# LayerNorm on channels: two transposes of the token's numbers in place of four transposes back

## The chip, the cores and the metric

The kernel runs on one core of one Trainium2 chip. A core has a matrix engine (TensorE, PE), three engines for elementwise work (VectorE or DVE, ScalarE or ACT, GpSimd or POOL) and SyncE (SP), which here issues all DMAs. PE writes to PSUM, eight banks of 128 partitions by 512 fp32 words; the others work mainly in SBUF. The metric is the device time of one execution in microseconds (us).

## What is computed

One layer of an encoder. 16 meta tokens stand ahead of the tokens; a prompt of 256 tokens and a sample of 2048 are handled as 18 blocks of 128. One projection makes the parts q, k, v, an attention gate, and for the convolution a value, a gate and an output gate, 512 channels each. The part that the change touches is this:

```
def layernorm(x, w, b):
    mu = jnp.mean(xf, axis=-1, keepdims=True)
    var = jnp.mean(jnp.square(xf - mu), axis=-1, keepdims=True)
    y = (xf - mu) * lax.rsqrt(var + LN_EPS)
    return y * w + b
def conformer_conv(c_val, c_glu, conv_w, conv_b, ln_w, ln_b):
    u = c_val * jax.nn.sigmoid(c_glu)
    y = lax.conv_general_dilated(u, conv_w, ...) + conv_b     # 31 taps, each channel by itself
    return jax.nn.silu(layernorm(y, ln_w, ln_b))              # over the 512 channels of a token
def hybrid_layer(z, ...):
    q, k, v, g_att, c_val, c_glu, g_conv = jnp.split(rmsnorm(z) @ w_in, ...)
    att = windowed_gqa(rmsnorm(q), rmsnorm(k), v, sink) * jax.nn.silu(g_att)
    cnv = conformer_conv(c_val, c_glu, ...) * jax.nn.silu(g_conv)
    return z + jnp.concatenate([att, cnv], axis=-1) @ w_out
```

## The kernel before

**Projection.** The columns of the input projection are cut into units of 256 (weights `ws`), the tokens into groups of 384 (group 0 has 400), and the groups into two chunks of three. Every product is made of three fp32r passes over high and low halves (`xh`, `xl`), so that one unit for one block of 128 tokens is 24 matmuls of 256 columns, `pj73` for instance (L879). Results go through eight PSUM banks under four tags, "a" to "d", with two banks each; a tag's tiles take its two banks in turn, in the order in which the program asks for them.

**Preparing a group of tokens.** The tokens of a group lie transposed in DRAM. Four loads on SP (L743, `xt4_0` to `xt4_3` for group 4) bring 256 channels each. The token's rstd is spread over the partitions by three transposes of a broadcast column (L755, `bc4`, PSUM tag "c"), eight DVE instructions multiply with it (L772, two for each load), ACT casts to `xh` (L791), and DVE and POOL make `xl` (L801). A load into a buffer waits for the `xl` of the group before.

**Convolution and LayerNorm.** DVE adds the 31 taps with the channels on the partitions (L937, L946), into four tiles `y{c}_{j}` of 128 channels each for chunk c. When a chunk is done, `ln_block` handles its blocks: 0 to 7 after chunk 0, 8 to 17 after chunk 1. For a block, step `s1` turns the four pieces of y to tokens on partitions (four transposes, `lnt`, tag "c", L221), DVE makes mean and variance (`bs`, L224; `mv`, L225), and POOL from these rstd and −mean·rstd, columns 1 and 2 of `mv` (L148, L149, L227). `s2` lets DVE write (y · rstd − mean · rstd) from PSUM to `zn` (L234). `s3` turns that back with four transposes (`lnu`, tag "d", or "a" in the attention phase, L240); ACT applies weight, bias and Silu per channel (L243), and SP stores the block to DRAM (`cd`, L246). The last block columns of chunk 0 wait in `ycarry` and are copied ahead of chunk 1's y by ACT.

**What sets the order.** The program goes through the projection's work items; after each, `tick` advances a clock, starts the next LayerNorm block or convolution taps for the time that PE has been given, and runs what `later(k, f)` put off by k ticks. The framework then orders the instructions of each engine itself by a simulated timeline (POOL, and in the attention phase PE, keep the program's order) and puts in the waits that data and buffers need. In a row each engine works strictly in order: an instruction that waits holds all behind it. q leaves PSUM through DVE (`qs`, L1010), and the splits of weights (L839, `wor` L345) run between.

Of the kernel before, what the change touches and what calls it, by code (L numbers as in the profile page):

```python
# [32 lines left out]
NJ = 4  # L33
# [66 lines left out]
def hymba_kernel(  # L100
# [11 lines left out]
    nc = tc.nc  # L112
# [3 lines left out]
    psum = ctx.enter_context(tc.tile_pool(name="psum", bufs=2, space=bass.MemoryType.PSUM))  # L116
# [45 lines left out]
    def later(k, f):  # L162
        due.setdefault(clock[0] + k, []).append(f)
# [45 lines left out]
    phase = [1]  # L209

    def ln_block(c, b, ready):
        if c == 0:
            o = P * b if b < NB_P else 286 + P * (b - NB_P)
        else:
            o = P * (b - 8)
        st = {}

        def s1():
            pt = psum.tile([P, 512], F32, tag="c", name=f"lnt{b}")
            for j in range(NJ):  # L220
                nc.tensor.transpose(pt[:, P * j : P * j + P], yt[c, j][:, o : o + P], ident)  # L221
            bs = yp.tile([P, 6], F32, tag="bs", name=f"bs{b}")
            mv = yp.tile([P, 3], F32, tag="mv", name=f"mv{b}")
            nc.vector.bn_stats(out=bs, in_=pt)  # L224
# [3 lines left out]
            st["pt"], st["mv"] = pt, mv  # L228
            later(1, s2)

        def s2():
            st["zn"] = yp.tile([P, 512], F32, tag="zn", name=f"zn{b}", bufs=3)
            mv = st["mv"]
            nc.vector.tensor_scalar(st["zn"], st["pt"], mv[:, 1:2], mv[:, 2:3], op0=ALU.mult, op1=ALU.add)  # L234
            later(1, s3)

        def s3():
            pt = psum.tile([P, 512], F32, tag="d" if phase[0] == 1 else "a", name=f"lnu{b}")
            for j in range(NJ):
                nc.tensor.transpose(pt[:, P * j : P * j + P], st["zn"][:, P * j : P * j + P], ident)  # L240
            cn = st["zn"].rearrange("p (j n) -> p j n", n=P)
            for j in range(NJ):
                nc.scalar.activation(  # L243
                    cn[:, j, :], pt[:, P * j : P * j + P], AF.Silu, bias=lb[:, j : j + 1], scale=lw[:, j : j + 1]
                )
            later(1, lambda: nc.sync.dma_start(cd[b], st["zn"]))  # L246

        ln_q.append((ready, s1))

# [450 lines left out]

    if True:
        rows0 = {}
        sq0 = yp.tile([P, YW], F32, tag="y", name="sq0")

        def pinned(op, yes=True):
            if yes:
# [2 lines left out]
        def stats(i):  # L709
            rows = NM if i == 0 else P  # L710
            r0 = 0 if i == 0 else NM + P * (i - 1)
            if i < 4:
                xn = cp.tile([P, UWID], F32, tag="us", name=f"xn{i}")[:, :D]
                rows0[i] = xn
            elif i == 4:
                xn = yp.tile([P, YW], F32, tag="y", name=f"xn{i}")[:, :D]
# [12 lines left out]
            return rest  # L729
# [78 lines left out]
        def weights(k):  # L808

            key = keys[k]  # L810
            raw = {}

            def load(eng):
                pool = wl if k % 2 else wr
                ws = pool.tile([P, ND, 2, UW], F32R, tag="ws", name=f"ws{key[0]}_{key[1]}")
                wsplit[key] = ws
                if key[0] == 1 and key[1] >= CACHE:
                    for q in range(4):
                        part = ws[:, 2 * q : 2 * q + 2].rearrange("p d a n -> p (d a n)")
# [104 lines left out]
        def conv(c, j, part):  # L924
            yo = 0 if c == 0 else YC
            o0, o1 = (0, YN)
            n = o1 - o0

            def alloc():
                yt[c, j] = yp.tile([P, YW], F32, tag="y", name=f"y{c}_{j}")  # L930
                if c == 1:
                    nc.scalar.copy(yt[c, j][:, 0:YC], ycarry[:, j, :])

            def tap(k):
                y, u = yt[c, j], us[c, j]
                if k == 0:
                    nc.vector.tensor_scalar(  # L937
                        y[:, yo + o0 : yo + o1],
                        u[:, o0:o1],
                        cw[:, j, 0:1],  # L940
                        cb[:, j : j + 1],
                        op0=ALU.mult,
                        op1=ALU.add,
                    )
# [370 lines left out]
```

## Time and profile before

| | |
|---|---|
| median of 3 runs | 943.38 us (943.36 to 943.39) |
| the profiled execution | 943.95 us; its span in the trace 941.9 us |
| PE busy | 935.6 us, 99% of the span |
| DVE, ACT, POOL busy | 744.4 us (79%), 421.8 us (45%), 293.3 us (31%) |
| moved by DMA | 176.49 MB, mean 187 GB/s |
| LayerNorm of blocks 0–7, of 8–17 | about 283 to 339 us, 531 to 577 us |

The page of the profile gives busy times per engine, then the span in 40 slices, the chain of work that ended last, and the costliest groups. In a row of groups, "out<-in" are the program's names without numbers, followed by a count and the durations; in a timeline row the first number is the start, the second how long the named instructions take together, and a bracket at the end says how long the engine had been idle and what ended it. Matmuls are pipelined: a matmul's duration is longer than its step to the next.

### The profile page before, as it was taken

To read this page: it belongs to the slowest core of one execution; us is meant where nothing else is said; L and a number is where in the kernel's file an instruction comes from. 1 tells how busy PE (TensorE), PEld (TensorE's weight loads), DVE (VectorE), ACT (ScalarE), POOL (GpSimd) and SP (SyncE) were. 2 spreads that over 40 slices of the span, in tenths; PEclk is the share of its full clock that TensorE was granted. 3 is DMA by queue.
4 is the path that set the end of the run, shared out by engine and by line. 5 is a ranking of instruction groups with operands and counts; after the bars stand their busy time and mean duration, and the time that the engine had idled before them with its cause. 6 is when DMAs were issued, how large, how long until landed. Compare 5 with 4: busy or idle time off the path is not lost.

```text
span 941.9 us, 16665 instructions
## 1 busy us (share of the span) xinstructions
PE 935.6 (99%) x5794; PEld 886.3 (94%) x5794; DVE 744.4 (79%) x1263; ACT 421.8 (45%) x1160; POOL 293.3 (31%) x490
## 2 busy tenths in 40 slices
PE   9999999999999999999999999999999999999998
PEld 8999999999999999999999999988888888888887
DVE  5579999997977879999996655677777677767773
ACT  7432022253457751011111356666666666656661
POOL 4320000173558400000000553755433242333332
PEclk9999999999999999999999999999999999999999
DMA  8575345676656595233333697975666556655512
GB/s 306 170 253 217 134 176 176 217 269 251 182 185 189 182 312 182 90 113 134 140 128 123 159 327 225 395 240 159 200 188 172 151 165 196 188 159 148 163 62 68
DMA packets 146211, 176.49 MB, mean 187 GB/s; under 512 B 40816, under 2 KB 108736, under 8 KB 146000
## 3 DMA queue, kind: packets, MB, share of 16 engines
q1 hardware_dynamic: 146128, 175.43, 57.8%
q8 instruction: 46, 0.75, 0.3%
q14 instruction: 37, 0.30, 0.1%
HBM read 112.69 MB, written 62.70 MB: 186 GB/s over the span
## 4 chain that ended last, share of the span: by engine, by line
PE 94%; DMA 2%; DVE 1%; SPq 1%; issue 0%; ACT 0%; POOL 0%; DVEq 0%; ACTq 0%; POOLq 0%
PE pj L863 43%; PE y L609 21%; PE pj L879 13%; PE O L533 5%; PE S L383 4%; PE pT_c L499 2%; PE pT_m L499 2%; PE pT_x L499 1%; DMA cd<-zn 1%; DMA bias<-in_bias_c 1%; PE qT L383 1%; PE lnu L240 0%; DMA xn<-in_z 0%; PE lnt L221 0%; DVE xt L772 0%
## 5 line engine op out<-in xcount | busy, mean ns | idle before, releaser
L863 PE MATMUL pj<-xh,ws 128*128 128x384 f32 (+1 forms) x1536 | 395.9, 338 | 0.1
L946 DVE SCALAR_TENSOR_TENSOR y<-us,cw,y 128x1167 f32<-128x1167 f32 x240 | 329.0, 1427 | 0.4
L863 PEld LDWEIGHTS pj<-xh,ws 128*128 128x128 f32 x1536 | 280.0, 188 | 0.4 <-ACT xh L1111 0.4
L863 PE MATMUL pj<-xl,ws 128*128 128x384 f32 (+1 forms) x768 | 260.9, 340 | 0.1
L609 PE MATMUL y<-wo,rest 128*128 128x512 f32 (+1 forms) x672 | 172.7, 394 | 0.0
L879 PE MATMUL pj<-ws,xh 128*128 128x256 f32 (+1 forms) x880 | 164.2, 284 | 0.3 <-DVE kn L1037 0.3
L863 PEld LDWEIGHTS pj<-xl,ws 128*128 128x128 f32 x768 | 144.1, 188 | 0.5 <-DVE xl L801 0.4
L609 PEld LDWEIGHTS y<-wo,rest 128*128 128x128 f32 x672 | 117.5, 189 | 21.4 <-DVE rest L566 0.3
L879 PEld LDWEIGHTS pj<-ws,xh 128*128 128x128 f32 (+1 forms) x880 | 136.1, 187 | 1.1 <-issue 0.4
L879 PE MATMUL pj<-ws,xl 128*128 128x256 f32 (+1 forms) x440 | 124.3, 283 | 0.0
L441 DVE CUSTOM_DVE_ANT_0 sb<-S,bias,vec 128x304 f32<-128x304 f32 (+5 forms) x144 | 74.5, 517 | 33.8 <-PE S L383 31.5
L453 ACT ACTIVATE sb<-sb,nm 128x304 f32<-128x304 f32 (+5 forms) x144 | 77.8, 540 | 48.9 <-DVE nm L441 48.2
L971 ACT ACTIVATE go<-pj 128x384 f32<-128x384 f32 x48 | 23.5, 489 | 149.8 <-PE pj L863 142.3
L879 PEld LDWEIGHTS pj<-ws,xl 128*128 128x128 f32 (+1 forms) x440 | 82.2, 187 | 0.2
L479 POOL TENSOR_SCALAR sb<-sb,es 128x304 f32<-128x304 f32 (+5 forms) x144 | 73.1, 525 | 16.0 <-DVE es L466 13.1
L561 POOL TENSOR_TENSOR at<-at,ga 128x256 f32<-128x256 f32 x36 | 26.5, 737 | 164.0 <-DVE at L555 104.8
L148 POOL TENSOR_SCALAR ssk<-ssk 128x2 f32<-128x2 f32 x18 | 8.4, 465 | 210.0 <-ACT sqk L985 210.0
L383 PEld LDWEIGHTS S<-kw,q 128*128 128x128 f32 x288 | 53.2, 188 | 10.6
L383 PE MATMUL S<-kw,q 128*128 128x304 f32 (+5 forms) x288 | 62.8, 299 | 0.0
L148 POOL TENSOR_SCALAR ssq<-ssq 128x4 f32<-128x4 f32 (+2 forms) x55 | 23.5, 427 | 98.3 <-ACT xn L726 74.4
L906 ACT ACTIVATE sg<-pj 128x384 f32<-128x384 f32 (+1 forms) x24 | 11.8, 492 | 82.9 <-PE pj L863 82.0
L609 PE MATMUL y<-wo,mch 128*128 128x512 f32 x144 | 47.2, 409 | 0.0
(139 smaller groups left out, 1306.9 us busy)
## 6 DMA issues: line engine op xcount, KB each, us to landing
wd<-ws SPq DMA_DIRECT2D x36, 512.0 KB, 5.8
ws<-wd SPq DMA_DIRECT2D x36, 512.0 KB, 6.2
wraw<-in_w_in SPq DMA_DIRECT2D x52, 256.0 KB, 6.3
xn<-in_z SPq DMA_DIRECT2D x18, 512.0 KB, 5.5
gd<-go SPq DMA_DIRECT2D x48, 192.0 KB, 2.2
yo<-in_z SPq DMA_DIRECT2D x36, 256.0 KB, 3.9
out_y<-yo SPq DMA_DIRECT2D x35, 256.0 KB, 2.7
wo<-wod SPq DMA_DIRECT2D x16, 512.0 KB, 7.4
```

The source lines that it names most:

```text
L148: nc.gpsimd.tensor_scalar(src, src, scale, eps, op0=ALU.mult, op1=ALU.add)
L383: r = f(*a, **k)
L441: nc.vector.tensor_tensor_reduce(out=sb[:, n, c0:c1], in0=ps[:, 0:w], in1=cst["bias"][:, kv, at + c0 : at + c1], scale=1.0, scalar=nsnk[:, ...
L453: nc.scalar.activation(sb[:, n, c0:c1], sb[:, n, c0:c1], AF.Exp, bias=nm[:, n : n + 1], scale=-1.0, accum_out=rs[:, n : n + 1],)
L479: nc.gpsimd.tensor_scalar(sb[:, k, a0:a1], sb[:, k, a0:a1], es[:, k : k + 1], 1.0, op0=ALU.mult, op1=ALU.mult)
L499: nc.tensor.transpose(pt[: c1 - c0, n, :], sbt[b, kv][:, n, c0:c1], ident)
L533: nc.tensor.matmul(opj[b, kv][:, n0:n1], t[:r, kv, :], p[:r, n0:n1], start=(k == "c" and i == 0), stop=(k == "x" and i == len(work) - 1),)
L561: nc.gpsimd.tensor_tensor(at[:, pr, :], at[:, pr, :], gat[b][:, pr, :], op=ALU.mult)
L609: nc.tensor.matmul(ps, mh[mi][:, e % 4, :], wo[e, wi][:, cols], start=(e == 4 and k == 0), stop=(e == 3 and k == 2),)
L863: nc.tensor.matmul(ps[:, :n], ws[:, d, wi, P * half_i : P * half_i + P], x[xi][:, d, o : o + n], start=(k == 0), stop=(k == 3 * ND - 1),)
L879: nc.tensor.matmul(ps[:rows, :UW], x[xi][:, d, o : o + rows], ws[:, d, wi, :], start=(k == 0), stop=(k == 3 * ND - 1),)
L946: nc.vector.scalar_tensor_tensor(y[:, yo + o0 : yo + o1], u[:, o0 + k : o1 + k], cw[:, j, k : k + 1], y[:, yo + o0 : yo + o1], op0=ALU.mul ...
```

## The change

The transposes back are dropped: the block stays with its channels on the partitions. After `s1`, which is as before, `s2` (two ticks later, so that `mv` is there) turns the two numbers of each token, each repeated over 128 columns, so that PSUM holds rstd and −mean·rstd along the tokens, the same in every partition (`lnu`, now 2 × 128 columns, L235). `s3` multiplies the four pieces of y in SBUF with the first (L241) and adds the second (L242), both on DVE over 512 columns with the PSUM operand repeated over the four pieces; then ACT applies Silu from SBUF to SBUF (L245) and the store follows one tick later. For this the four y tiles become one, `ybig`, which also serves the early tiles that used the same buffers. The second chunk's y thus takes the place of the first's while blocks are still read from it.

```
-    yt = {}
+    ybig = yp.tile([P, NJ, YW], F32, tag="y", name="ybig", bufs=1)
...
-                nc.tensor.transpose(pt[:, P * j : P * j + P], yt[c, j][:, o : o + P], ident)
+                nc.tensor.transpose(pt[:, P * j : P * j + P], ybig[:, j, o : o + P], ident)
...
-            later(1, s2)
+            later(2, s2)
         def s2():
-            st["zn"] = yp.tile([P, 512], F32, tag="zn", name=f"zn{b}", bufs=3)
-            mv = st["mv"]
-            nc.vector.tensor_scalar(st["zn"], st["pt"], mv[:, 1:2], mv[:, 2:3], op0=ALU.mult, op1=ALU.add)
+            st["pt"] = psum.tile([P, 2, P], F32, tag="d" if phase[0] == 1 else "a", name=f"lnu{b}")
+            for k in range(2):
+                nc.tensor.transpose(st["pt"][:, k, :], st["mv"][:, k + 1 : k + 2].to_broadcast([P, P]), ident)
             later(1, s3)
         def s3():
-            pt = psum.tile([P, 512], F32, tag="d" if phase[0] == 1 else "a", name=f"lnu{b}")
+            zn = yp.tile([P, NJ, P], F32, tag="zn", name=f"zn{b}", bufs=3)
+            wide = [st["pt"][:, k, :].unsqueeze(1).to_broadcast([P, NJ, P]) for k in range(2)]
+            nc.vector.tensor_tensor(zn, ybig[:, :, o : o + P], wide[0], op=ALU.mult)
+            nc.vector.tensor_tensor(zn, zn, wide[1], op=ALU.add)
             for j in range(NJ):
-                nc.tensor.transpose(pt[:, P * j : P * j + P], st["zn"][:, P * j : P * j + P], ident)
-            cn = st["zn"].rearrange("p (j n) -> p j n", n=P)
-            for j in range(NJ):
-                nc.scalar.activation(
-                    cn[:, j, :], pt[:, P * j : P * j + P], AF.Silu, bias=lb[:, j : j + 1], scale=lw[:, j : j + 1]
-                )
-            later(1, lambda: nc.sync.dma_start(cd[b], st["zn"]))
+                nc.scalar.activation(zn[:, j, :], zn[:, j, :], AF.Silu, bias=lb[:, j : j + 1], scale=lw[:, j : j + 1])
+            later(1, lambda: nc.sync.dma_start(cd[b], zn.rearrange("p j n -> p (j n)")))
...
-        flush(max(0, 4 - clock[0] + ln_at[0]))
+        flush(max(0, 5 - clock[0] + ln_at[0]))
```

The order that the framework finds changes with it. Three places follow; block numbers stand behind lnt, lnu, zn and bs, group numbers behind bc, xt and xl, and the number after an underscore only tells tiles apart.

**PE, group 4's spreading of rstd in the first LayerNorm stretch.** Before, it stands late in pj73, behind the transposes back of block 0:

```order
L879 MATMUL pj73_3199<-ws0_7_2507,xl1_371 128x256
L879 MATMUL pj73_3199<-ws0_7_2507,xh1_370 128x256 x2
L240 MATMUL lnu0_3087<-ident_72,zn0_3034 128x128 x4
L755 MATMUL bc4_3104<-ident_72,rstd_86 128x128 x3
L879 MATMUL pj73_3199<-ws0_7_2507,xl1_371 128x256
L879 MATMUL pj73_3199<-ws0_7_2507,xh1_370 128x256
```

After, it stands in the first matmuls of pj72, right behind block 1's first transposes:

```order
L879 MATMUL pj71_3029<-ws0_7_2500,xl1_368 128x256
L879 MATMUL pj71_3029<-ws0_7_2500,xh1_367 128x256
L222 MATMUL lnt1_3063<-ident_72,ybig_108 128x128 x2
L879 MATMUL pj72_3107<-ws0_7_2500,xh1_367 128x256
L755 MATMUL bc4_3089<-ident_72,rstd_86 128x128 x3
L879 MATMUL pj72_3107<-ws0_7_2500,xl1_368 128x256
L879 MATMUL pj72_3107<-ws0_7_2500,xh1_367 128x256 x2
```

So bc4 has moved up by almost two units of 24 matmuls. Its tile is the third of tag "c" in both, after lnt0 and lnt1; its bank is lnt0's.

**PE and DVE around lnt3.** On PE before, lnt2 and lnt3 stand after pj75, with lnu1 between them:

```order
L879 MATMUL pj75_3341<-ws0_7_2507,xh2_481 128x256
L221 MATMUL lnt2_3158<-ident_72,y0_0_680 128x128
L221 MATMUL lnt2_3158<-ident_72,y0_1_770 128x128
L221 MATMUL lnt2_3158<-ident_72,y0_2_1350 128x128
L221 MATMUL lnt2_3158<-ident_72,y0_3_1524 128x128
L240 MATMUL lnu1_3186<-ident_72,zn1_3122 128x128 x4
L221 MATMUL lnt3_3233<-ident_72,y0_0_680 128x128
L221 MATMUL lnt3_3233<-ident_72,y0_1_770 128x128
L221 MATMUL lnt3_3233<-ident_72,y0_2_1350 128x128
L221 MATMUL lnt3_3233<-ident_72,y0_3_1524 128x128
L879 MATMUL pj76_3414<-ws0_7_2507,xh2_481 128x256
```

After, lnt2 stands ahead of pj73 and lnt3 between pj73 and pj74:

```order
L879 MATMUL pj73_3180<-ws0_7_2500,xl1_368 128x256
L879 MATMUL pj73_3180<-ws0_7_2500,xh1_367 128x256
L222 MATMUL lnt3_3214<-ident_72,ybig_108 128x128 x4
L235 MATMUL lnu1_3168<-ident_72,mv1_3069 128x128 x2
L879 MATMUL pj74_3244<-ws0_7_2500,xh2_478 128x256
```

lnt3 takes bc4's bank, so it follows the last DVE instruction that reads bc4. Those on DVE before are:

```order
L234 TENSOR_SCALAR zn0_3034<-lnt0_3017,mv0_3023 128x512
L1010 TENSOR_TENSOR qs1_2_3032<-pj70_2983,rqq1_2_3014 128x256
L772 SCALAR_TENSOR_TENSOR xt4_0_2932<-xt4_0_2932,vec_77,bc4_3104 128x384 x2
L772 SCALAR_TENSOR_TENSOR xt4_1_2934<-xt4_1_2934,vec_77,bc4_3104 128x384 x2
L1010 TENSOR_TENSOR qs1_3_3120<-pj71_3038,rqq1_3_3069 128x256
L772 SCALAR_TENSOR_TENSOR xt4_2_2936<-xt4_2_2936,vec_77,bc4_3104 128x384
L234 TENSOR_SCALAR zn1_3122<-lnt1_3072,mv1_3078 128x512
L772 SCALAR_TENSOR_TENSOR xt4_2_2936<-xt4_2_2936,vec_77,bc4_3104 128x384
L772 SCALAR_TENSOR_TENSOR xt4_3_2938<-xt4_3_2938,vec_77,bc4_3104 128x384 x2
```

and after:

```order
L772 SCALAR_TENSOR_TENSOR xt4_0_2925<-xt4_0_2925,vec_77,bc4_3089 128x384 x2
L772 SCALAR_TENSOR_TENSOR xt4_1_2927<-xt4_1_2927,vec_77,bc4_3089 128x384 x2
L225 BN_STATS bs2_3146<-lnt2_3141 128x6
L772 SCALAR_TENSOR_TENSOR xt4_2_2929<-xt4_2_2929,vec_77,bc4_3089 128x384 x2
L241 TENSOR_TENSOR zn0_3171<-ybig_108,lnu0_3078 128x512
L226 BN_AGGR mv2_3147<-bs2_3146 128x2
L1010 TENSOR_TENSOR qs1_2_3025<-pj70_2976,rqq1_2_3007 128x256
L772 SCALAR_TENSOR_TENSOR xt4_3_2931<-xt4_3_2931,vec_77,bc4_3089 128x384 x2
```

The eight readers of bc4 (L772) start the row now, and bs2, the multiplication of zn0 and qs1_2 stand between their pairs.

**PE and DVE around lnt6.** On PE before, lnt6 follows lnt5 and lnu4 after several units more; after, eight matmuls and lnu4 stand between lnt5 and lnt6, which takes the bank of bc5:

```order
L222 MATMUL lnt5_3354<-ident_72,ybig_108 128x128
L879 MATMUL pj76_3392<-ws0_7_2500,xl2_479 128x256
L879 MATMUL pj76_3392<-ws0_7_2500,xh2_478 128x256 x2
L879 MATMUL pj76_3392<-ws0_7_2500,xl2_479 128x256
L879 MATMUL pj76_3392<-ws0_7_2500,xh2_478 128x256 x2
L879 MATMUL pj76_3392<-ws0_7_2500,xl2_479 128x256
L879 MATMUL pj76_3392<-ws0_7_2500,xh2_478 128x256
L235 MATMUL lnu4_3379<-ident_72,mv4_3284 128x128 x2
L222 MATMUL lnt6_3426<-ident_72,ybig_108 128x128 x4
```

The readers of bc5 on DVE stand together before:

```order
L224 BN_STATS bs4_3303<-lnt4_3298 128x6
L225 BN_AGGR mv4_3304<-bs4_3303 128x2
L772 SCALAR_TENSOR_TENSOR xt5_0_3112<-xt5_0_3112,vec_77,bc5_3329 128x384 x2
L772 SCALAR_TENSOR_TENSOR xt5_1_3114<-xt5_1_3114,vec_77,bc5_3329 128x384 x2
L772 SCALAR_TENSOR_TENSOR xt5_2_3116<-xt5_2_3116,vec_77,bc5_3329 128x384 x2
L772 SCALAR_TENSOR_TENSOR xt5_3_3118<-xt5_3_3118,vec_77,bc5_3329 128x384 x2
L234 TENSOR_SCALAR zn4_3339<-lnt4_3298,mv4_3304 128x512
```

and after, bs5 (which reads lnt5), zn3's multiplication and qs1_5 stand ahead of the last pair:

```order
L772 SCALAR_TENSOR_TENSOR xt5_1_3099<-xt5_1_3099,vec_77,bc5_3310 128x384 x2
L772 SCALAR_TENSOR_TENSOR xt5_2_3101<-xt5_2_3101,vec_77,bc5_3310 128x384 x2
L225 BN_STATS bs5_3359<-lnt5_3354 128x6
L241 TENSOR_TENSOR zn3_3382<-ybig_108,lnu3_3291 128x512
L1010 TENSOR_TENSOR qs1_5_3240<-pj73_3180,rqq1_5_3211 128x256
L772 SCALAR_TENSOR_TENSOR xt5_3_3103<-xt5_3_3103,vec_77,bc5_3310 128x384 x2
```

So the last pair has moved behind an instruction that needs lnt5.

More of the change, by code (lines that the diff above doesn't have):

```diff
@@ L207, in hymba_kernel @@
     cp = right_pools.enter_context(tc.tile_pool(name="cp", bufs=4, side="right"))
-    yt = {}
+    ybig = yp.tile([P, NJ, YW], F32, tag="y", name="ybig", bufs=1)
     phase = [1]
+    normed = [0]
     def ln_block(c, b, ready):
@@ L227, in s1 @@
             nc.gpsimd.tensor_scalar(mv[:, 2:3], mv[:, 0:1], mv[:, 1:2], -1.0, op0=ALU.mult, op1=ALU.mult)
-            st["pt"], st["mv"] = pt, mv
-            later(1, s2)
+            st["mv"] = mv
+            later(2, s2)
         def s2():
-            st["zn"] = yp.tile([P, 512], F32, tag="zn", name=f"zn{b}", bufs=3)
-            mv = st["mv"]
-            nc.vector.tensor_scalar(st["zn"], st["pt"], mv[:, 1:2], mv[:, 2:3], op0=ALU.mult, op1=ALU.add)
+            st["pt"] = psum.tile([P, 2, P], F32, tag="d" if phase[0] == 1 else "a", name=f"lnu{b}")
+            for k in range(2):
+                nc.tensor.transpose(st["pt"][:, k, :], st["mv"][:, k + 1 : k + 2].to_broadcast([P, P]), ident)
             later(1, s3)
         def s3():
-            pt = psum.tile([P, 512], F32, tag="d" if phase[0] == 1 else "a", name=f"lnu{b}")
-            for j in range(NJ):
-                nc.tensor.transpose(pt[:, P * j : P * j + P], st["zn"][:, P * j : P * j + P], ident)
-            cn = st["zn"].rearrange("p (j n) -> p j n", n=P)
-            for j in range(NJ):
-                nc.scalar.activation(
-                    cn[:, j, :], pt[:, P * j : P * j + P], AF.Silu, bias=lb[:, j : j + 1], scale=lw[:, j : j + 1]
-                )
-            later(1, lambda: nc.sync.dma_start(cd[b], st["zn"]))
+            zn = yp.tile([P, NJ, P], F32, tag="zn", name=f"zn{b}", bufs=3)
+            wide = [st["pt"][:, k, :].unsqueeze(1).to_broadcast([P, NJ, P]) for k in range(2)]
+            nc.vector.tensor_tensor(zn, ybig[:, :, o : o + P], wide[0], op=ALU.mult)
+            nc.vector.tensor_tensor(zn, zn, wide[1], op=ALU.add)
+            normed[0] += 1
+            for j in range(NJ):
+                nc.scalar.activation(zn[:, j, :], zn[:, j, :], AF.Silu, bias=lb[:, j : j + 1], scale=lw[:, j : j + 1])
+            later(1, lambda: nc.sync.dma_start(cd[b], zn.rearrange("p j n -> p (j n)")))
         ln_q.append((ready, s1))
@@ L702, in hymba_kernel @@
         rows0 = {}
-        sq0 = yp.tile([P, YW], F32, tag="y", name="sq0")
+        sq0 = ybig[:, 0]
         def pinned(op, yes=True):
@@ L715, in stats @@
             elif i == 4:
-                xn = yp.tile([P, YW], F32, tag="y", name=f"xn{i}")[:, :D]
+                xn = ybig[:, 1, :D]
             else:
@@ L824, in load @@
                         if q % 2 == 0:
-                            pair = yp.tile([P, YW], F32, tag="y", name=f"wraw{k}_{q}")
+                            pair = ybig[:, 2 + q // 2]
                         raw[q] = pair[:, 512 * (q % 2) : 512 * (q % 2) + 512].rearrange("p (a n) -> p a n", n=UW)
@@ L929, in alloc @@
             def alloc():
-                yt[c, j] = yp.tile([P, YW], F32, tag="y", name=f"y{c}_{j}")
                 if c == 1:
-                    nc.scalar.copy(yt[c, j][:, 0:YC], ycarry[:, j, :])
+                    assert normed[0] == 8
+                    nc.scalar.copy(ybig[:, j, 0:YC], ycarry[:, j, :])
             def tap(k):
-                y, u = yt[c, j], us[c, j]
+                y, u = ybig[:, j], us[c, j]
                 if k == 0:
```

## The prediction

> **What bounds the kernel now.** I read the page's engine table, clock row and chain first.
>
> ```profile
> PE 935.6 (99%) x5794; PEld 886.3 (94%) x5794; DVE 744.4 (79%) x1263; ACT 421.8 (45%) x1160; POOL 293.3 (31%) x490
> PEclk9999999999999999999999999999999999999999
> PE 94%; DMA 2%; DVE 1%; SPq 1%; issue 0%; ACT 0%; POOL 0%; DVEq 0%; ACTq 0%; POOLq 0%
> ```
>
> TensorE (PE) is busy for 935.6 of 941.9 us at full granted clock, and the chain that ended last is 94% PE. So the time falls only by PE work that goes away and rises by every new wait of PE; what is added on DVE or ACT counts only where PE waits for it. Next the waits of PE and the table by stretches: LayerNorm runs at 283–340 us (blocks 0–7) and at 531–577 us (blocks 8–17).
>
> ```profile
> PE warmup L1096 <- POOL ident masks.py:199: 1.4, 1, 1.4
> PE lnu L240 <- DVE zn L234: 0.7, 1, 0.7
> 283.00:300.00 17.00, 17.00 (x146) 16.87 (x146) 12.51 (x25) 13.60 (x64) 14.85 (x22) 1.00 0.50 150
> 300.00:312.00 12.00, 12.00 (x86) 11.97 (x84) 9.04 (x19) 9.65 (x28) 8.26 (x15) 1.00 0.63 202
> 312.00:340.00 28.00, 28.00 (x172) 27.86 (x171) 19.78 (x35) 22.31 (x48) 8.23 (x16) 1.00 0.68 227
> 560.00:580.00 20.00, 19.30 (x164) 18.91 (x164) 9.24 (x20) 11.28 (x32) 8.23 (x20) 1.00 0.73 231
> ```
>
> The columns after the length are PE, PEld, DVE, ACT and POOL busy, clock and DMA share. PE has no gap in the first LayerNorm stretch (17.00 of 17, 12.00 of 12, 28.00 of 28); in the second it loses 0.7 us once, where the transposes back wait for DVE. DVE is 71–75% busy in the first.
>
> **The change, part by part.** The prices of the pieces, from the groups by tile:
>
> ```profile
> L221 PE MATMUL lnt<-ident,y x72: 271/272/273, 230.2 to 568.5; 128*128 128x128 f32 x72
> L240 PE MATMUL lnu<-ident,zn x72: 270/272/327, 292.2 to 575.6; 128*128 128x128 f32 x72
> L755 PE MATMUL bc<-ident,rstd x15: 270/272/273, 27.2 to 311.4; 128*128 128x128 f32 x15
> L224 DVE BATCH_NORM_STATS2 bs<-lnt x18: 668/695/701, 284.1 to 569.4; 128x6 f32<-128x512 f32 x18
> L234 DVE TENSOR_SCALAR zn<-lnt,mv x18: 777/810/811, 289.9 to 574.3; 128x512 f32<-128x512 f32 x18
> L516 DVE TENSOR_TENSOR ptiles<-pT_c,ptiles x36: 679/686/693, 593.2 to 923.4; 128x512 fp32r<-128x512 f32 x36
> L1010 DVE TENSOR_TENSOR qs<-pj,rqq x8: 415/424/426, 283.7 to 310.1; 128x256 f32<-128x256 f32 x8
> L243 ACT ACTIVATE zn<-lnu,vec x72: 447/457/490, 292.9 to 576.9; 128x128 f32<-128x128 f32 x72
> ```
>
> *Transposes.* Per block four transposes back (L240) go and two of a number spread over 128 columns come. L755 is the same form as the new ones and takes the same 272 ns. But matmuls are pipelined; what one costs PE is its step to the next, and the timeline gives that:
>
> ```profile
> 286.59 0.38 PE L221 MATMUL lnt<-ident,y 128*128 128x128 f32 x2
> 292.22 0.60 PE L240 MATMUL lnu<-ident,zn 128*128 128x128 f32 x4
> 292.66 0.49 PE L755 MATMUL bc<-ident,rstd 128*128 128x128 f32 x3
> 299.08 0.60 PE L221 MATMUL lnt<-ident,y 128*128 128x128 f32 x4
> 299.52 0.60 PE L240 MATMUL lnu<-ident,zn 128*128 128x128 f32 x4
> 299.95 0.60 PE L221 MATMUL lnt<-ident,y 128*128 128x128 f32 x4
> 575.22 0.63 PE L240 MATMUL lnu<-ident,zn 128*128 128x128 f32 x4 [0.66 <-DVE zn L234]
> ```
>
> Four start at 292.22 and the next group at 292.66: 0.109 us each. 72 − 36 = 36 fewer, so 36 × 0.109 = **−3.92 us**, all on the bound. The last row is the 0.66 us wait for zn; the new transposes need only `mv`, ready before any store of `cd` matters, so I take **−0.66 us** (its bounds are −0.66 and 0, if the next PE work inherits the wait).
>
> *DVE, ACT, POOL.* Per block one tensor_scalar (0.81) becomes two tensor_tensor of 512 columns; the nearest row with a PSUM operand is L516, 0.69. So +0.57 us per block, 10 us in all, beside PE in stretches where DVE has 25% idle: nothing by itself. ACT's Silu reads SBUF instead of PSUM: 0.457 now, not on PE's path, nothing. The store of `cd`, one tick later, stands on SP behind the loads of xt5; DVE waits for it only when a buffer of zn comes round. If that idle time were gone, the 10 us would be PE's. The single tile for y makes ACT's copies of the carry wait for zn0's multiplication, and the casts of xh4 stand behind them; PE reads xh4 only after lnt6, so they have over 10 us. Chunk 1's convolution may now start only when the last block of chunk 0 has been multiplied:
>
> ```profile
> 338.18 0.88 DVE L937 TENSOR_SCALAR y<-us,cw,vec 128x1167 f32<-128x1167 f32 x1
> 514.75 0.29 DVE L1029 TENSOR_TENSOR vs<-pj,vs 128x128 fp32r<-128x128 f32 x1 [9.07 <-ACT vs L1028]
> ```
>
> Its first tap is at 338.18 now; in the new DVE row it stands behind both steps of zn7 and some of W_out's splits, and I take 3 us later. Its cover is the 9.07 us that DVE idles before 514.75, with taps still to come: enough even for 3 + 4.6 = 7.6.
>
> *The order on PE in chunk 0.* Here the change adds waits. The bank of lnt0 used to be held until zn0 was made; now bn_stats frees it, so bc4 (group 4's rstd spread over channels, same two banks, tag "c") moves up from behind lnu0 to behind lnt1, and lnt2 and lnt3 move up too. The banks go round lnt0, lnt1, bc4, lnt2, lnt3, lnt4, bc5, lnt5, lnt6: lnt3 takes bc4's bank and must wait for the last of its eight readers (L772), and these need the loads of xt4.
>
> ```profile
> L743 SPq DMA_DIRECT2D xt<-in_zt x1: 368/368/368, 289.7 to 289.7; - x1
> DMA to landing us min/median/max: 4.1/4.1/4.1
> ...
> L743 SPq DMA_DIRECT2D xt<-in_zt x1: 368/368/368, 290.9 to 290.9; - x1
> DMA to landing us min/median/max: 3.9/3.9/3.9
> ...
> L743 SPq DMA_DIRECT2D xt<-in_zt x1: 368/368/368, 302.7 to 302.7; - x1
> DMA to landing us min/median/max: 4.7/4.7/4.7
> ...
> 289.86 1.01 POOL L801 TENSOR_TENSOR xl<-xt,xh 128x384 fp32r<-128x384 f32 x1
> 296.87 1.66 DVE L772 SCALAR_TENSOR_TENSOR xt<-xt,vec,bc 128x384 f32<-128x384 f32 x3
> 311.81 4.28 DVE L772 SCALAR_TENSOR_TENSOR xt<-xt,vec,bc 128x384 f32<-128x384 f32 x8
> ```
>
> The third load lands at 289.7 + 4.1 = 293.8, the fourth at 290.9 + 3.9 = 294.8; each is issued when POOL's xl (it ends 290.87) frees the buffer, in work that the change leaves alone. Eight L772 take 4.28 us; with 0.61 for one, the step is (4.28 − 0.61) / 7 = 0.524, so 0.09 less than the duration; I take the same off every DVE instruction but the last. From 293.8 the new DVE row is: two L772 (1.05), zn0's multiplication (0.60), an aggregate (0.1), qs (0.33), two L772 (0.52 + 0.61) = 3.2: lnt3 can start at 297.0. PE wants it earlier. Between lnt1 (286.59) and lnu0 (292.22) stand two transposes and 46 matmuls, (5.63 − 0.22) / 46 = 0.118 each; in the new order two transposes, 48 matmuls, then bc4's 3, lnu0's 2 and lnt2's 4 lead to lnt3: 286.59 + 11 × 0.109 + 48 × 0.118 = 293.45. **+3.6 us.** Below: the loads alone, 294.8 + 1.13 − 293.45 = 2.5; above: if one load takes as long as xt5's last (4.7), 4.4. Today the same eight end at 296.87 + 1.66 = 298.5, lnt3 stands at 299.95, and PE waits for nothing.
>
> [...]
>
> *The second wait.* lnt6 takes bc5's bank. In the new DVE order the last two L772 of xt5 stand behind bs5 (which needs lnt5), zn3's multiplication and qs: 0.61 + 0.60 + 0.33 + 0.52 + 0.61 = 2.7 us from lnt5's end. PE has 8 matmuls and 2 transposes in that time, 8 × 0.118 + 2 × 0.109 = 1.16. **+1.5 us**, whatever the loads do. Below 1.0, if each of the five steps overlaps the next by another 0.1. Above 2.5, if xt5's last load comes 1 us after the pair's turn; I expect it before, since it is issued when the later xl4 free the buffers, at about 303.4, and 4.7 more is 308.1, while lnt5 ends near 307.1 and the pair's turn is at 308.6. Before, the eight stand together at 311.81 and lnt6 comes much later.
>
> Sum: 943.95 (the profiled run; its span 941.9 and 2.05 around it) − 3.92 − 0.66 + 3.6 + 1.5 = 944.5. The median of the runs is 0.57 below the profiled run, so **943.9 us**. In words: two waits for one pair of PSUM banks eat the whole gain.
>
> **The rivals.** Measurement cannot tell less than about 0.2%, 1.9 us, from no change: 941.5 and 945.3 are the borders.
>
> *Neither wait binds* (chance 0.16): DVE gets to the pairs sooner than I read, or the banks go round otherwise. For it: PE never waited there before. Against it: the landings are rows, and the banks go round in the order in which the program asks for them. Time 943.38 − 4.58 = 938.8.
>
> *The first wait at its low end, no second* (0.14): 943.38 − 4.58 + 2.5 = 941.3, on the border.
>
> *TensorE cools in the wait* (slower, 0.12). At the start the same transposes are slow for a while:
>
> ```profile
> 1.36 4.63 PE L1096 MATMUL warmup<-ident 128*128 128x128 f32 x20 [1.36 <-POOL ident masks.py:199]
> 6.51 1.38 PE L1096 MATMUL warmup<-ident 128*128 128x128 f32 x10
> ```
>
> Twenty in 4.63 us, about 0.21 each against 0.12 for the ten after 6.51 (the granted clock of the page does not show it). A PE that stands still long enough would start so again: 20 × (0.213 − 0.109) = 2.1 us more, 946.0. It decides if 3.6 us without work is long enough; after the 0.66 us at 575.22 the next matmuls step at full speed, and no longer pause is in the trace. [...]
>
> *Further waits* (slower, 0.16): chunk 1's zn now takes two DVE steps behind stores of `cd` in a stretch at 0.73 DMA share, and chunk 1's convolution starts later. If lnu16 or the first scores take over the 0.66 us and add one more pair of 0.69, or the 9.07 us do not cover it: 1.5 to 4 us, 945.4 to 948.
>
> **How the numbers follow.** My forecast, both waits and nothing else, has 0.42: no change. Faster: the first rival and half of the second, 0.16 + 0.07 = 0.23. Slower: the third and fourth, and 0.04 of the forecast with both waits at their upper ends, 0.32. Same: the rest, 0.45. The range leaves out most of the first rival and the top of the last: 940.0 to 947.2.
>
> **What would show it.** Right: PE waits gain a row lnt <- DVE xt L772 of 2.5 to 4.4 us near 293.5 and a second of about 1.5 near 308; lnt and lnu matmuls count 72 and 36; PE busy falls by about 3.9; the two zn steps are near 0.69 each; the row lnu <- zn is gone. Wrong: no PE wait above 1 us in 283–312, or new waits after 531 us, or PE matmuls stepping at 0.2 us after a wait.

## The result: slower by 0.83%, 951.7 us

The changed kernel takes 951.70 us (median of 4 runs, 949.36 to 951.87) against 943.37 us before (943.02 to 943.39): ratio 1.0083, 95% interval 1.0067 to 1.0099. The forecast was 943.9 and the range ended at 947.2. The profiled execution of the changed kernel took 949.36 us, its span is 947.6. Of the kernels below, e2, e8 and e10 each had one run far above the rest (2380.5, 1313.0 and 1306.9 us), which their times and ratios leave out.

The engine table, the clock and the chain of the page after:

```profile
PE 935.5 (99%) x5758; PEld 884.3 (93%) x5758; DVE 753.8 (80%) x1281; ACT 421.6 (44%) x1158; POOL 293.2 (31%) x490
PEclk9999999999999999999999999999999999999999
PE 88%; DMA 5%; DVE 3%; SPq 1%; ACT 1%; issue 1%; POOL 1%; DVEq 0%; ACTq 0%; POOLq 0%
```

PE is as busy as before (935.5 against 935.6 us) although 36 matmuls fewer are counted, the clock row in tenths shows nothing, and the chain's share of PE fell from 94% to 88%: it now goes through DMA, DVE, POOL and ACT. The waits of PE (us in total, times, longest):

```profile
PE lnt L222 <- DVE bs L225: 1.2, 1, 1.2
PE lnu L235 <- POOL mv L149: 1.1, 1, 1.1
PE lnu L235 <- POOL mv L228: 0.9, 1, 0.9
PE S L383 <- DVE zn L242: 0.8, 1, 0.8
PE pj L879 <- DVE qs L1010: 0.5, 1, 0.5
```

How far the kernel lags behind is read from instructions that are the same in both: the last Silu of a gate in the projection (ACT, `go<-pj`) and the last addition of the output (DVE, `yo`). The rows give first and last start, two of before and then two of after:

```profile
L971 ACT ACTIVATE go<-pj x48: 472/491/493, 121.7 to 511.1; 128x384 f32<-128x384 f32 x48
...
L620 DVE TENSOR_TENSOR yo<-y,yo x37: 424/681/693, 620.8 to 938.7; 128x512 f32<-128x512 f32 x35, 128x256 f32<-128x256 f32 x2
```

```profile
L971 ACT ACTIVATE go<-pj x48: 471/492/496, 121.8 to 515.2; 128x384 f32<-128x384 f32 x48
...
L620 DVE TENSOR_TENSOR yo<-y,yo x37: 425/681/693, 626.2 to 944.2; 128x512 f32<-128x512 f32 x35, 128x256 f32<-128x256 f32 x2
```

Less the 0.06 us by which it was late at the first of these, the lag grows by 4.1 us net up to the last `go<-pj`, which I put down to chunk 0's LayerNorm, and by 1.2 from there to the end, put down to chunk 1's. Taking the changes of PE work out (−1.74 and −2.18 for the transposes, −0.66 for the old wait), the new losses are 5.9 and 4.1 us. The stretches of chunk 0, with PE, PEld, DVE, ACT, POOL busy, granted clock, DMA share, GB/s:

```profile
293.40:296.40 3.00, 1.40 (x9) 0.77 (x7) 2.57 (x7) 0.40 (x3) 2.82 (x5) 1.00 0.33 116
296.40:300.00 3.60, 3.58 (x17) 3.58 (x18) 3.60 (x8) 3.60 (x14) 3.12 (x7) 0.53 0.25 77
306.00:312.00 6.00, 4.58 (x34) 4.10 (x33) 5.99 (x13) 5.80 (x22) 5.49 (x10) 1.00 0.66 237
```

Two things stand there: from 293.4 to 296.4 PE has little to do, and **from 296.4 to 300.0 its granted clock is 0.53**. The timeline of PE, then the rows of DVE and POOL that belong to it:

```profile
293.43 0.28 PE L879 MATMUL pj<-ws,xh 128*128 128x256 f32 x1
293.86 0.66 PE L222 MATMUL lnt<-ident,ybig 128*128 128x128 f32 x4
294.35 0.27 PE L235 MATMUL lnu<-ident,mv 128*128 128x128 f32 x1
295.56 0.32 PE L235 MATMUL lnu<-ident,mv 128*128 128x128 f32 x1 [0.94 <-POOL mv L228]
296.42 0.57 PE L879 MATMUL pj<-ws,xh 128*128 128x256 f32 x1 [0.54 <-DVE qs L1010]
...
309.77 0.66 PE L222 MATMUL lnt<-ident,ybig 128*128 128x128 f32 x4 [1.16 <-DVE bs L225]
```

```profile
293.11 0.69 DVE L225 BATCH_NORM_STATS2 bs<-lnt 128x6 f32<-128x512 f32 x1
294.23 1.14 DVE L772 SCALAR_TENSOR_TENSOR xt<-xt,vec,bc 128x384 f32<-128x384 f32 x2 [0.43 <-DMA xt<-in_zt]
295.98 0.39 DVE L1010 TENSOR_TENSOR qs<-pj,rqq 128x256 f32<-128x256 f32 x1
296.29 1.13 DVE L772 SCALAR_TENSOR_TENSOR xt<-xt,vec,bc 128x384 f32<-128x384 f32 x2
...
293.33 0.55 POOL L149 TENSOR_TENSOR mv<-mv,half 128x1 f32<-128x1 f32 x1
293.84 1.03 POOL L149 TENSOR_TENSOR rqq<-ssq,half 128x4 f32<-128x4 f32 x1
295.24 0.27 POOL L228 TENSOR_SCALAR mv<-mv 128x1 f32<-128x1 f32 x1
```

lnt3 starts at 293.86, right after bs2 (293.11 + 0.69). lnu1's second transpose waits until 295.56 for the third column of mv1, which POOL makes at 295.24 behind a 1.03 us instruction for q. pj74 then waits until 296.42 for qs1_2, which frees its bank; on DVE that stands behind the readers of bc4, which wait for xt4's third load until 294.23. Six transposes are 0.65 us of work in the 2.9 us from pj73's end to pj74: 2.2 us lost. pj74's first 16 matmuls take 3.53 us (296.42 to 299.95) in place of 16 × 0.118 = 1.89: 1.6 us lost to the clock. lnt6 waits 1.2 us for bs5. That is 5.0 of the 5.9 us.

Chunk 1, in which a chain runs from a store of `cd` through DVE to PE; DVE first, then POOL, then PE:

```profile
569.11 0.69 DVE L241 TENSOR_TENSOR zn<-ybig,lnu 128x512 f32<-128x512 f32 x1 [3.60 <-DMA cd<-zn]
570.11 0.68 DVE L242 TENSOR_TENSOR zn<-zn,lnu 128x512 f32<-128x512 f32 x1
...
564.24 0.27 POOL L228 TENSOR_SCALAR mv<-mv 128x1 f32<-128x1 f32 x1
...
570.93 0.40 PE L235 MATMUL lnu<-ident,mv 128*128 128x128 f32 x2 [1.06 <-POOL mv L149]
582.91 0.45 PE L383 MATMUL S<-kw,q 128*128 128x208 f32 x2 [0.77 <-DVE zn L242]
```

zn14's multiplication waits 3.6 us for a zn buffer whose block is still being stored, so its second step, which also reads lnu14, ends only at 570.11 + 0.68 = 570.79. lnu16 takes lnu14's bank and starts at 570.93, after 1.06 us in which PE is idle. The bracket names POOL's power (L149), which ended last before it, but that one, at 570.33, is block 17's: block 16's numbers are complete at 564.24 + 0.27 = 564.51, 6.4 us before. At 582.91 the scores wait for the second step of the last zn, whose multiplication had waited 1.1 us for a store. In all PE is idle for 3.2 us between 515 and 620, so 0.9 of chunk 1's 4.1 us is not placed.

### The profile page after: what moved, and what is told of

The parts are those of the page before. It is cut to its first block, busy times and chain, and to the rows that moved or that the text cites. A ratio compares the mean times of both kernels' runs of the same rounds, so it can differ in the third digit from the quotient of the medians.

```text
span 947.6 us, 16600 instructions
## 1 busy us (share of the span) xinstructions
PE 935.5 (99%) x5758; PEld 884.3 (93%) x5758; DVE 753.8 (80%) x1281; ACT 421.6 (44%) x1158; POOL 293.2 (31%) x490
## 4 chain that ended last, share of the span: by engine, by line
PE 88%; DMA 5%; DVE 3%; SPq 1%; ACT 1%; issue 1%; POOL 1%; DVEq 0%; ACTq 0%; POOLq 0%
PE pj L863 42%; PE y L609 21%; PE pj L879 9%; PE O L533 5%; PE S L383 4%; PE pT_c L499 2%; PE pT_m L499 2%; PE pT_x L499 1%; DMA cd<-zn 1%; DMA cn<-cd 1%; DMA vc<-vd 1%; PE qT L383 1%; DMA kd<-ks 1%; DVE xt L772 1%; DMA qd<-qr 1%
## 5 line engine op out<-in xcount | busy, mean ns | idle before, releaser
L863 PE MATMUL pj<-xh,ws 128*128 128x384 f32 (+1 forms) x1536 | 396.5, 339 | 0.4 <-DVE qs L1010 0.3
L946 DVE SCALAR_TENSOR_TENSOR ybig<-us,cw,ybig 128x1167 f32<-128x1167 f32 x240 | 328.9, 1426 | 0.4
L863 PEld LDWEIGHTS pj<-xh,ws 128*128 128x128 f32 x1536 | 280.0, 188 | 1.1 <-DVE qs L1010 0.5
L863 PE MATMUL pj<-xl,ws 128*128 128x384 f32 (+1 forms) x768 | 260.8, 340 | 0.1
L879 PE MATMUL pj<-ws,xh 128*128 128x256 f32 (+1 forms) x880 | 167.6, 287 | 0.8 <-DVE qs L1010 0.5
L863 PEld LDWEIGHTS pj<-xl,ws 128*128 128x128 f32 x768 | 144.1, 188 | 0.6 <-DVE xl L801 0.4
L879 PEld LDWEIGHTS pj<-ws,xh 128*128 128x128 f32 (+1 forms) x880 | 138.3, 188 | 1.7 <-DVE qs L1010 0.7
L879 PE MATMUL pj<-ws,xl 128*128 128x256 f32 (+1 forms) x440 | 124.6, 283 | 0.0
L879 PEld LDWEIGHTS pj<-ws,xl 128*128 128x128 f32 (+1 forms) x440 | 83.0, 189 | 0.2
```

The source lines that it names most:

```text
L863: nc.tensor.matmul(ps[:, :n], ws[:, d, wi, P * half_i : P * half_i + P], x[xi][:, d, o : o + n], start=(k == 0), stop=(k == 3 * ND - 1),)
L879: nc.tensor.matmul(ps[:rows, :UW], x[xi][:, d, o : o + rows], ws[:, d, wi, :], start=(k == 0), stop=(k == 3 * ND - 1),)
L946: nc.vector.scalar_tensor_tensor(y[:, yo + o0 : yo + o1], u[:, o0 + k : o1 + k], cw[:, j, k : k + 1], y[:, yo + o0 : yo + o1], op0=ALU.mul ...
```

## The experiments

Lag is against the trace of before, from the same two rows, less the lag at the first `go<-pj`; "chunk 0" and "chunk 1" are net, so that the saving (−1.74, −2.18) is in them. There is one trace of before, and equal stretches of two traces of the changed kernel differ by up to 0.9 us. Ratios are to the runs of before on the same chip, in which before itself lay between 942.9 and 945.8.

| kernel | chunk 0 | chunk 1 | span | time | before beside it | ratio, interval |
|---|---|---|---|---|---|---|
| changed | +4.14 | +1.23 | 947.6 | 951.70 | 943.37 | 1.0083 (1.0067–1.0099) |
| after_2, after_3 | +4.57, +5.05 | +1.43, +2.11 | 948.2, 950.1 | 950.25, 952.14 | 943.67 | one run each |
| e1_fill | +1.92 | +1.98 | 946.2 | 947.60 | 944.03 | 1.0037 (1.0022–1.0051) |
| e2_c0back | +1.00 | +1.95 | 944.8 | 946.86 | 944.03 | 1.0028 (1.0018–1.0039) |
| e3_c1back | +4.86 | −1.14 | 945.5 | 948.06 | 944.03 | 1.0047 (1.0032–1.0062) |
| e5_bc3 | +0.39 | +0.25 | 943.1 | 946.74 | 944.03 | 1.0026 (1.0015–1.0036) |
| e6_zn6 | +5.30 | +0.24 | 947.9 | 950.09 | 943.91 | 1.0070 (1.0055–1.0085) |
| e7_bc3zn6 | +0.31 | +1.29 | 943.8 | 945.36 | 943.91 | 1.0016 (1.0006–1.0026) |
| e8_oldctrl | +1.07 | −0.34 | 942.7 | 944.72 | 943.91 | 1.0009 (1.0000–1.0019) |
| e4_mean | −0.29 | −0.77 | 940.9 | 944.58 | 943.67 | 1.0008 (0.9998–1.0018) |
| e9_mean | −0.74 | −1.07 | 940.2 | 941.99 | 943.91 | 0.9983 (0.9970–0.9996) |
| e10_mean3 | −0.74 | +1.25 | 943.3 | 944.43 | 943.67 | 1.0006 (0.9995–1.0016) |

### One chunk at a time (e2_c0back, e3_c1back)

In e2 the blocks of chunk 0, in e3 those of chunk 1, go the old way, on the single tile:

```
+            if c == 0:            # e3: c == 1
+                later(1, s2_back)   # tensor_scalar from PSUM, then s3_back: four transposes, Silu
+            else:
                 later(2, s2)
```

> The changed kernel in which the blocks of chunk 0 are handled in the old way (tensor_scalar from PSUM one tick later, four transposes back), on the new single y tile; chunk 1 as changed. Theory A (chunk 0 costs a net 4.1 us, because of the order of its waits): the time is before + 1.2 us, 944.6, and PE waits near 294 and 309 are gone. Theory B (the single tile or the later convolution start costs the time): still 947 or more, with the lag at 340 us as before.

> The changed kernel in which the blocks of chunk 1 are handled in the old way; chunk 0 as changed. Theory A (chunk 0 costs 4.1 us net, chunk 1 1.2 us net): before + 4.1, 947.5, with the waits and the slow clock at 293 to 300 us as in the changed kernel, and no wait of S for zn. If the runs of the changed kernel at 951.7 owe their extra 2.3 us to chunk 1, this one is steady at 947.5; if they owe it to chunk 0, it goes to 949 to 950.

The losses follow the part: 3.1 of chunk 0's 4.1 go with e2, and with e3 chunk 1 is 1.1 us ahead of before. e3's time is 4.0 us above before, where 4.1 was expected, though one run reached 950.25. PE waits in 560–620 for nothing any more in e3:

```profile
560.00:620.00 60.00, 60.00 (x478) 58.09 (x477) 36.54 (x103) 38.83 (x113) 31.01 (x69) 1.00 0.92 325
```

e2 keeps one wait in chunk 0, pj74 for qs1_2 (0.92 us), so the new tile and the new order cost something there with the old LayerNorm too; e2 is 2.8 us above the before beside it, not 1.2. Theory B is refuted for most of the loss, not for that microsecond.

### Filling the wait (e1_fill), and the clock in three traces

```
+                if b == 1 and k == 0:
+                    for i in range(10):
+                        nc.tensor.transpose(st["pt"][:, 2 + i % 2, :], ident, ident)
```

> The changed kernel with ten extra transposes of the identity (128 columns, results unused) between the two transposes of block 1's numbers, where PE waits for mv1. Theory A (a stretch of 3 us in which PE does six transposes makes the clock drop): the extra work of 10 x 0.109 = 1.1 us fits into the wait, the granted clock of the following 3.6 us is 1.0 instead of 0.53, pj74's matmuls step at 0.118 us instead of 0.213, and the time falls by about 1.5 to 1.7 us. Theory B (the slow matmuls come from the wait for q or from a shared port, not from idleness): the clock row there stays near 0.5 and the time does not fall. The order behind this place also changes (lnt6 moves), which both theories allow another 1 us for.

```profile
293.40:296.40 3.00, 2.54 (x23) 1.00 0.29 103
296.40:300.00 3.60, 3.60 (x34) 1.00 0.30 99
300.00:312.00 12.00, 10.75 (x80) 1.00 0.69 217
```

The ten transposes, 1.1 us of idle work, made chunk 0 2.2 us shorter: the clock is 1.0 after them. The time fell by 4.1 us, not by 1.5 to 1.7. But the order behind it changed as well (no wait of lnt6 for bs5), and the next two traces show that the clock can stay at 1.0 there without them, so this run does not show that the filling did it.

> The changed kernel once more, one look. Theory A (the slow stretch is the clock, and depends on where a wait falls in time, not on the program alone): the waits near 294 and 309 come back at the same places and lengths within 0.5 us, but the stretch with granted clock 0.50 of about 3.5 us may follow the first, the second, both or none; the span is 945.5 with none, 947.3 with one, 949 with two, and this is why the runs lay between 949.4 and 951.9. Theory E (the slow stretch belongs to the instructions after lnu1): it is at 296.4 to 300 again.

> As after_2, a third look at the changed kernel; the two theories say the same of it.

Each trace of the changed kernel has one slow spell, at a clock of 0.50 and 3.41 us long. The rows show PE in pieces of that length, cut so that the spell is one of them, with busy PE time, number of matmuls, granted clock, DMA share and GB/s; first the profiled run of the result, then after_2 and after_3:

```profile
293.05:296.47 3.42, 1.80 (x13) 1.00 0.38 120
296.47:299.88 3.41, 3.41 (x16) 0.50 0.26 81
```

```profile
292.16:295.58 3.42, 2.54 (x21) 1.00 0.45 138
305.82:309.23 3.41, 0.75 (x6) 1.00 0.77 272
309.23:312.64 3.41, 3.38 (x13) 0.50 0.29 99
```

```profile
307.28:310.70 3.42, 1.06 (x6) 1.00 0.63 233
310.70:314.11 3.41, 3.25 (x10) 0.50 0.23 77
570.11:573.52 3.41, 1.67 (x15) 1.00 1.00 304
```

In after_2 and after_3 the spell follows the second wait (2.2 us there), and the same matmuls behind the first run at 1.0. So it belongs to no instruction: theory E falls. e3 and e6 have the same mean clock as these three over 283–320, 0.95. In the rows above, the pieces before a spell held 13, 6 and 6 matmuls; behind those with 21 (2.54 us busy) and 15 (1.67) the clock stays at 1.00. Other stretches with little work were not followed by a spell either: in the profiled run of the result, 308.60 to 312.01 held 12 matmuls and the clock is 1.00 up to 317, and in e2 PE was busy for 1.71 of the 4 us from 566 to 570, with the wait of lnu16 in it, and the clock is 1.00 from 564 to 576. What decides behind which stretch a spell comes was not shown.

All six runs of the changed kernel have a mean clock of 0.998, which one spell gives (1 − 0.5 × 3.41 / 948), so my explanation of their spread of 949.4 to 952.1 fails: after_3 lost its 2.5 us against the profiled run in other places (0.7 at the start, 0.9 in each chunk). In other kernels the mean clock does change from run to run: two runs of e6 and the slowest of e9 (947.26) have 0.996, as two spells would give (1 − 2 × 0.5 × 3.41 / 948), and the slowest runs of e2 and e7 have 0.998 where their profiled runs have 1.000.

### Group rstd two ticks later (e5_bc3)

```
-                    later(1, p.first)
+                    later(3, p.first)
-                        later(1 + q // 2, lambda p=p, q=q: p.scale(q))
+                        later(3 + q // 2, lambda p=p, q=q: p.scale(q))
```

> The changed kernel in which the spreading of rstd for groups 3 to 5 (bc4 and its eight readers) is asked for two ticks later, so that on DVE the four instructions for q (qs1_2) and zn0 stand ahead of the readers that wait for xt4's loads. Theory A (the readers, moved up, hold DVE for the loads, and q's PSUM bank and so pj74 wait behind them): no PE wait over 0.5 us and no slow clock in 290 to 300; chunk 0's net cost falls from +4.1 to between -1.7 and -0.3; time 941.5 to 944.5. Theory B (mv from POOL is late whatever the readers do): the wait of lnu1 for mv stays at about 1 us and the clock drops again; time 947 or more.

```profile
293.40:296.40 3.00, 3.00 (x28) 1.00 0.74 212
296.40:300.00 3.60, 3.60 (x33) 1.00 0.32 114
300.00:312.00 12.00, 11.18 (x84) 1.00 0.68 203
```

With q's instruction ahead of the readers of bc4, PE is busy through the whole stretch at full clock, and chunk 0 falls from +4.14 to +0.39. Theory A's chain holds, its size does not: the expected −0.3 or less was not reached, and the time of 946.74 lies 2.2 us above the expected range (the trace is the fastest of eight runs, 945.03). The 0.8 us that are left at 300–312 are another wait for q (`PE pj L863 <- DVE qs L1010: 0.8`). The edit also sets lnu1's two transposes apart (295.01 and 297.25, with matmuls of pj between), so it does not say what the wait for q and the wait for POOL are worth singly.

### Six buffers for zn (e6_zn6), both (e7_bc3zn6), and the control (e8_oldctrl)

```
-            zn = yp.tile([P, NJ, P], F32, tag="zn", name=f"zn{b}", bufs=3)
+            zn = yp.tile([P, NJ, P], F32, tag="zn", name=f"zn{b}", bufs=6)
```

> The changed kernel with six buffers for zn instead of three, so that DVE's multiplication need not wait for an older block's store to cd. Theory C (chunk 1's loss: the aggregate of block 16 stands on DVE behind the multiplication of block 13, which waits for a buffer still being stored; POOL, then PE's lnu16 and the first scores wait after it): DVE waits no more for cd<-zn, PE's waits for mv L149 and for zn L242 near 570 and 582 go, chunk 1 goes from +1.2 us to about -2, and the lag at the end from +5.4 to 2 to 3 us. Theory D (the lag of chunk 1 comes from the crowded DMA queues or from two DVE steps in place of one): lnu16 still waits, and the lag stays near 5. The waits of chunk 0 stay under both.

> Both moves together: the spreading of rstd two ticks later and six buffers for zn. If theories A and C are right and their parts add: chunk 0 +0.4 us as with the later spreading alone, chunk 1 about -2: a span 1.5 to 2 us below before, with no PE wait over 0.8 us after the start. If the single y tile or DVE's load has a cost of its own, the span stays at before's or above.

> The kernel before (four transposes back) with the same two moves: the control for them. If the moves only mend what the change broke, this one is within 1 us of before (its only related wait is 0.7 us near 575, which the buffers may take away). If they are worth something by themselves, it gains as much as the changed kernel does, and the change itself is worth nothing.

In e6 DVE's wait for the store is gone, and so are those of lnu16 for mv and of S for zn; chunk 1 falls by 1.0 us, not by 3: new waits took their place.

```profile
PE lnt L222 <- DVE bs L225: 2.8, 1, 2.8
PE pj L879 <- ACT sqq L980: 0.9, 1, 0.9
PE S L383 <- DVE nm L441: 0.7, 1, 0.7
```

So C names the start of the chain, the store, rightly, its middle wrongly (the bank, not the aggregate and POOL) and its price too: the lag at the end stays at 5.5 us, not 2 to 3. e7 shows that the two edits don't add: its chunk 1 is worse than e5's, and its span is 1.9 us above before's, not 1.5 to 2 below. e8 says that they are worth nothing to the old LayerNorm (+0.7 us by the lag).

### Mean and rstd in place of rstd and −mean·rstd (e4_mean, e9_mean, e10_mean3)

```
-            nc.gpsimd.tensor_scalar(mv[:, 2:3], mv[:, 0:1], mv[:, 1:2], -1.0, op0=ALU.mult, op1=ALU.mult)
-                nc.tensor.transpose(st["pt"][:, k, :], st["mv"][:, k + 1 : k + 2].to_broadcast([P, P]), ident)
+                nc.tensor.transpose(st["pt"][:, k, :], st["mv"][:, k : k + 1].to_broadcast([P, P]), ident)
+            nc.vector.tensor_tensor(zn, ybig[:, :, o : o + P], wide[0], op=ALU.subtract)
+            nc.vector.tensor_tensor(zn, zn, wide[1], op=ALU.mult)
```

> The changed kernel with mean and rstd spread in place of rstd and -mean*rstd, and neither of the two moves. If POOL's last step was what held PE (lnu1 for mv L228, lnu16 for mv L149), the waits for mv go and the time falls by 2 us or more, to 947 or less. If the readers of bc4 that wait for xt4's loads on DVE hold q's bank anyway, pj74 still waits for qs until about 296 and the gain in chunk 0 is under 1 us.

> Both moves and, in addition, mean and rstd are spread instead of rstd and -mean*rstd, so that zn is (y - mean) * rstd and POOL's last step per block (L228, 0.27 us and its place in POOL's row) falls away. If what is left in chunk 0 is the wait for POOL's numbers, the span is a further 0.3 to 1 us below the one with both moves; if what is left is the wait for q or for loads, the two are equal within 0.3 us.

> Mean and rstd spread, the later spreading of group rstd, but three buffers for zn as in both kernels. If the six buffers help once the numbers come early, this one is 0.5 us or more behind the one with six; if they only reshuffle the order of chunk 1 (with rstd and -mean*rstd the six cost 0.8 us), the two are equal or this one is ahead, a span of 939.5 to 940.5.

The mean comes straight from DVE's aggregate, rstd one POOL step earlier. In its trace (e4) this edit alone takes 6.4 us off the lag (from +5.37 to −1.06) and leaves no wait of PE for mv; pj74 still waits 0.7 us for q, as expected, yet chunk 0 gained 4.4 us, not under 1: the wait is short, the clock stays at 1.00 and lnt6 does not wait. The order on PE changed with the edit (lnu1's transposes stand at 290.76 and 293.71), so the gain is that of the formula with the order that follows from it. Its runs reach from 942.9 to 947.65, with a median that cannot be told from before: the trace is one of the faster ones. With both moves and six buffers, e9 is the only kernel that is faster than before, by 0.17% (0.04 to 0.30%); its span is 3.6 us below e7's, where 0.3 to 1 was expected. The end of the output in its trace, and its stretches:

```profile
L619 DVE TENSOR_TENSOR yo<-y,yo x37: 423/680/692, 619.1 to 937.1; 128x512 f32<-128x512 f32 x35, 128x256 f32<-128x256 f32 x2
...
293.40:300.00 6.60, 6.60 (x59) 1.00 0.53 185
300.00:312.00 12.00, 12.00 (x89) 1.00 0.65 192
560.00:580.00 20.00, 20.00 (x173) 1.00 0.81 251
```

With three buffers (e10) chunk 1 loses 2.3 us against e9, and the wait again begins at a store: zn14's multiplication waits for it on DVE, and the aggregate with lnu16's mean stands behind that. PE first, then DVE:

```profile
566.47 0.29 PE L234 MATMUL lnu<-ident,mv 128*128 128x128 f32 x1 [1.42 <-DVE mv L226]
...
563.70 0.69 DVE L240 TENSOR_TENSOR zn<-ybig,lnu 128x512 f32<-128x512 f32 x1 [5.81 <-DMA cd<-zn]
...
566.15 0.17 DVE L226 BATCH_NORM_AGGREGATE mv<-bs 128x2 f32<-128x6 f32 x1
```

Three buffers need not cost this: e4 has three too, its DVE waits up to 3.9 us for a store, and its chunk 1 is 0.77 us ahead of before. That fits a wait for a store that costs only where PE is due for what stands behind it; what six buffers are worth by themselves is open.

## Why the prediction was wrong, step by step

- **Transposes, −3.92 us: right in number and price.** 36 `lnu` and 72 `lnt` are in the trace, 0.272 us each. No kernel shows the whole saving: in e9, whose PE is busy throughout 293.4–312, chunk 0 is ahead by 0.74 of the 1.74 us, and the rest is not placed. PE busy did not fall by 3.9, as I said it would, since the matmuls around the waits and in the slow spell take longer (the page's L879 with `xh`: 164.2 to 167.6 us).
- **The old wait, −0.66 us: the wait went, a longer one came.** "the new transposes need only `mv`, ready before any store of `cd` matters" is the step that failed in chunk 1, and it is the largest miss: they also need a PSUM bank, which lnu14 holds until zn14's second step, and that stands on DVE behind a multiplication that waits for a store. I priced chunk 1 only under "further waits", at 1.5 to 4 us with 0.16; it measured 4.1 us of new losses, 1.8 of them the two waits shown. The DVE row of before has such waits for stores too (8.4 us in all), but they cost PE only 0.66.
- **The first wait, +3.6 us: there, for another reason.** I let lnt3 wait for the last reader of bc4. It waited for bs2, so it took lnt2's bank: the two banks of tag "c" were not taken in turn here, which I had assumed (lnt3 starts at 293.86, bs2 ends at 293.80). What held PE at that place was POOL's third column of mv1 and then q's bank behind the same readers, which I had in DVE's row but followed only to lnt3, not to pj74. Lost: 2.2 us. e5, which moves those readers behind q, removes both waits; e4, which leaves the readers and makes the numbers earlier, removes the first and keeps 0.7 us of the second. So both links count, and neither run gives one its own price. (The upper bound that I gave, 4.4, is 4.15 by its own rows: 289.7 + 4.7 + 3.2 − 293.45.)
- **The second wait, +1.5 us: right in size and place** (1.16 us at 309.77, 2.2 in the other two traces), again by another bank: lnt6 waits for bs5, lnt5's reader, not for the last pair of L772.
- **The clock, a rival with 0.12 and 2.1 us: it is what happened**, with 1.6 us in the profiled run. I let it hang on whether 3.6 us without work is long enough; but PE did 13 matmuls in the 3.42 us before the spell, and no single gap in them reached 1.2 us. The warmup rows that I called the same transposes are plain matmuls with the identity.
- **DVE, +10 us hidden beside PE: right** (744.4 to 753.8 us busy); the two steps take 0.683 and 0.676 us against the 0.69 I took.
- **The profile, 0.57 us above the median: the other way round.** The profiled run of the changed kernel is 2.3 us below its median, so the sum from the trace (5.4 us) is less than the 8.3 us between the medians. Two more runs gave 950.25 and 952.14; what differs between runs is spread over several waits, and why they differ is open.

The profiled run is 4.9 us above my sum of 944.5: the first wait −1.4 (2.2 in place of 3.6), the second −0.3, the clock +1.6, chunk 1 +4.1, and +0.9 in chunk 0 that I have not placed. These add up because the losses are read from the lag. I had weighed the clock and chunk 1 as rivals of which one might come; both came together.

## What to carry to other kernels

Where the bound engine has no gap, count work that is taken off it at no more than its step (here 0.109 us for a transpose that takes 0.272), and at that only if what is left finds its operands and its buffer ready: follow each new operand, and the buffer that it is written to, back through each engine's row (here POOL for mv's third column, DVE for the last reader of the bank) to the DMA at its end. An instruction that moves up in a row with one early operand can hold what stands behind it until its late operand lands: here the readers of bc4 waited for xt4's third load until 294.23, qs1_2 behind them started at 295.98, and pj74 at 296.42. And of two equal formulas, try the one whose operands are made first: (y − mean)·rstd in place of y·rstd − mean·rstd was worth 6 us in the trace here.

## What the hardware showed that was not expected

TensorE's granted clock fell to 0.50 for 3.41 us once in each of the three traces of the changed kernel, which have two stretches of little PE work about 13 us apart: behind the first of them in the profiled run of the result (from 296.47), behind the second in after_2 (from 309.23) and after_3 (from 310.70). The 3.41 to 3.42 us before the spell held 13, 6 and 6 matmuls; 12 matmuls in 308.60–312.01 of the first of these traces were followed by none. What sets a spell off was not shown. The slice row of the page, in tenths over 24 us, hides the spell (it shows 9 throughout); windows of 1 to 3 us do show it.
